# A two-layer decoder trunk on one core: the decay's inputs as columns ahead of the values', and stated places for k_d, low parts and adaLN dots

## The chip, the cores and the metric

The kernel runs on one core of a Trainium2 chip. The metric is the device time of one execution in microseconds (us). The engines are TensorE (PE; its weight loads are listed as PEld), VectorE (DVE), ScalarE (ACT), GpSimd (POOL) and SyncE (SP), which issues nearly all DMAs. Each engine runs its own instructions in a fixed order, and waits on semaphores for the others.

## The reference, cut to what matters

A trunk of two layers over 256 tokens of width 1024. Layer 0 mixes tokens by dilated window attention, layer 1 by gated linear attention; each is followed by a gated convolutional feed-forward part. Ahead of each sub-layer stands an RMSNorm whose shift, scale and gate come from a conditioning vector (adaLN: `silu(c) @ w_ada + b_ada`). The change lies in layer 1's mixer:

```python
def gla_mixer(h, w_in, w_gate, b_gate, g_norm, w_out):
    proj = h @ w_in                                  # q, k: 512 each, v: 1024, glr: 16, r: 1024
    ...
    gk = jax.nn.log_sigmoid((glr @ w_gate + b_gate).astype(jnp.float32)) / B_TAU
    ...
    bcum = jnp.cumsum(gk, axis=3)                    # within chunks of 64 tokens
    blast = bcum[:, :, :, -1:, :]
    q_t = q * jnp.exp(bcum)
    k_t = k * jnp.exp(-bcum)
    k_d = k * jnp.exp(blast - bcum)
    A = jnp.where(causal, jnp.einsum('bhncd,bhnsd->bhncs', q_t, k_t), 0.0)
    o_intra = jnp.einsum('bhncs,bhnse->bhnce', A, v)
    kv = jnp.einsum('bhncd,bhnce->bhnde', k_d, v)
    ...                                              # state over chunks: s = decay * s + kv
    o = o_intra + jnp.einsum('bhncd,bhnde->bhnce', q_t, s_prev)
    ...                                              # per head: rmsnorm(o) * silu(r), then @ w_out
```

There are four heads (key width 128, value width 256) and four chunks of 64 tokens.

## The kernel before

**Number format.** Large products run in F32R. Each float32 operand is split into a high part, a cast of it, and a low part, the rest. `mm3` (L196) makes one product of three: high × high, low × high, high × low (L199 to L201). `split` (L161) loads a weight piece into one of four raw buffers, casts the high parts on ScalarE (L172, tile whi, three buffers) and subtracts for the low parts on VectorE (L178, tile wlo, three buffers), each in two halves. Its arguments `after`, `low` and `late` name instructions behind which a half must stand.

**Order.** The program is recorded once; a scheduler then puts the instructions of each engine in order by its own estimate of times. `behind(...)` states that something must stand behind named instructions; everything else is the scheduler's. The order is fixed when the kernel runs.

**adaLN.** `next_ada` (L457) takes the next chunk of w_ada: one DMA of 1 MB into a raw buffer and two dots on VectorE (L140: one long operation and one that reads the accumulator), each followed by a small operation on ScalarE. The chunks in layer 1's mixer are for the feed-forward part behind it.

**Layer 1's mixer.** The normed input h stands as eight row blocks (kt) of 128 × 256, with a high part (hhi) and a low part (hlo) each; `all_normed` makes them from kt 0 to kt 7, while the first products already run. Then:

- *Values* (L1089 to L1109): the weight w_v_b comes in four pieces of two row blocks each, all 1024 columns wide. For each row block, each half of the tokens (t) and each half of the columns (s) there is an `mm3` into one of four PSUM banks pv[t][s].
- *Decay* (`log_gates`, L1045): behind the second piece a small weight w_glr (16 columns, padded) is split, and eight `mm3` give the 16 inputs as rows (tile glr, 16 × 256). `gates_of` (L1055) multiplies them by w_gate in plain float32, one product for each head (tile z), and makes log-sigmoid (nz, ea, sp), the running sum within chunks (cs), its distance from the chunk's end (dl), and the exponentials e_q, e_k, e_d and dec. It runs once for head 0 alone and once for heads 1 to 3 together.
- *Heads* (`states`, L1114): `mm3`s give q and k (bank pqk; for head 0 only k, since its q was made early), VectorE makes k_d, q_t and k_t, k_d is transposed (bank kdt) and copied (kdT), then come the masked scores (a, a_t) and three products kv, from which the states st follow. q_t, k_t, k_d have two buffers each, so head 3 takes those of head 1.
- *Outputs* (`products`, L1182, and `normed_output`, L1196): twenty small products (bank o) from a_t, v, q_t and st, their squares (osq, oacc), a mean over the head (ms, a product with a constant), and the normalised output on.
- *Output gate* (`gate`, L1211): four pieces of w_r_b (bank pr).

The order in which these are recorded:

```python
    s0 = states(0)
    s1 = states(1)
    output(0, *s0)
    s2 = states(2)
    po1 = products(1, *s1)
    s3 = states(3)
    normed_output(1, po1, last_a)
    po2 = products(2, *s2)
    gate(0)
    for _ in range(3):
        next_ada()
    po3 = products(3, *s3)
```

`last_a` is the last product of the scores, here head 3's: ms of head 1 stands behind it.

Of the kernel before, what the change touches and what calls it, by code (L numbers as in the profile page):

```python
# [57 lines left out]
def trunk(ctx: ExitStack, tc: tile.TileContext, I, out):  # L58
# [103 lines left out]
    def split(src, n, dmas=1, after=((), ()), late=(), low=(), lows=True):  # L162
# [5 lines left out]
        lo = wspl.tile([P, 2048], F32R, tag="wlo", name="wlo")  # L168
        for i in range(0, n, n // 2):
            c = slice(i, i + n // 2)  # L170
            with behind(*after[i > 0]):
                copied[0] = nc.scalar.copy(hi[:, c], raw[:, c])  # L172
        if not lows:
            return hi, lo, raw, n // 2
        for i in range(0, n, n // 2):
            c = slice(i, i + n // 2)
            with behind(*(late if i else low)):
                last_lo[0] = nc.vector.tensor_tensor(lo[:, c], raw[:, c], hi[:, c].bitcast(F32), op=ALU.subtract)  # L178
        return hi, lo
# [276 lines left out]

    def next_ada():  # L457
        if rest:
            ada_chunk(*rest.pop(0))

# [578 lines left out]
    nc.sync.dma_start(causal, I["causal"])  # L1039
    w_g = gt([16, 512], "w_g")  # L1040
    nc.sync.dma_start(w_g, I["w_gate"])

    glr_copy = []

    def log_gates():  # L1045
        with behind(*chain[5]):
            w_gl = split(I["w_glr"], 7 * 16 + P)
        ps = bank("glr", "t")
        for kt in range(KT):
            mm3(ps[:, :T], parts(w_gl, 16 * kt), h[kt], kt == 0, kt == KT - 1)  # L1050
        glr = gt([16, T], "glr")
        glr_copy.append(nc.vector.tensor_copy(glr, ps[:16, :T]))
        return [gates_of(*part, glr) for part in PARTS]

    def gates_of(first, n, glr):  # L1055
        def new(name, tag, columns=n * T):
            return gt([P, columns], name, tag=f"{tag}{min(first, 1)}")

        nz = new("nz", "A")
        for i in range(n):  # L1060
            hd = first + i
            ps = bank("z", "sttt"[hd])
            mm(ps[:, :T], w_g[:, P * hd : P * hd + P], glr, start=True, stop=True)
            nc.scalar.activation(nz[:, T * i : T * i + T], ps[:, :T], AF.Identity,
                                 scale=-1.0, bias=nbg[:, hd : hd + 1])
# [12 lines left out]
        dl = new("dl", "C")  # L1078
        nc.vector.tensor_tensor(dl.rearrange("p (n c) -> p n c", c=CH), cs3,
                                last.to_broadcast([P, 4 * n, CH]), op=ALU.subtract)  # L1080
# [9 lines left out]
    for n in range(4):  # L1090
        with behind(*((), chain[5], chain[7], glr_copy)[n]):
            w = split(I["w_v_b"][n], 2048) if n else w_first
            if n > 1:
                next_ada()
        if n == 0:
            with behind(*chain[7]):
                whole(early_q)
        for i in range(2):
            kt = 2 * n + i
            for t in range(2):  # L1100
                ht = [y[:, P * t : P * t + P] for y in h[kt]]
                for s in range(2):
                    mm3(pv[t][s], ht, parts(w, D * i + 512 * s, 512), kt == 0, kt == KT - 1)
        if n == 1:
            gates = log_gates()
    v = [gt([P, D], f"v{t}") for t in range(2)]
    for t in range(2):
        nc.scalar.copy(v[t][:, 0:512], pv[t][0])
        nc.vector.tensor_copy(v[t][:, 512:D], pv[t][1])  # L1109

    o_n = []
    last_a, last_sq, copies, kept = [None], [None], [None], [None, None]

    def states(hd):  # L1114
        if hd == 0:
# [5 lines left out]
        else:  # L1121
            w = split(I["w_qk_b"][hd], 2048)
            pqk = bank("pqk", "p")
# [10 lines left out]
        nc.vector.scalar_tensor_tensor(q_t, pq, P ** -0.5, e_q[:, c], op0=ALU.mult, op1=ALU.mult)  # L1134
        nc.vector.tensor_tensor(k_t, pk, e_k[:, c], op=ALU.mult)

        ps = bank("kdt", "t")
        kd = gt([P, T], "kdT", bufs=2)
        for t in range(2):
            c = slice(P * t, P * t + P)  # L1140
            nc.tensor.transpose(ps[:, c], k_d[:, c], ident)
        nc.scalar.copy(kd, ps[:, :T])
# [14 lines left out]
        vh = slice(T * hd, T * hd + T)  # L1157
        st = []
        kv = bank("kv", "t")
        for n in range(3):  # L1160
            t, r = n // 2, slice(CH * (n % 2), CH * (n % 2) + CH)
            d = (kv[:, :T], ps[:, T:], kv[:, T:])[n]
            last = mm(d, kd[r, P * t : P * t + P], v[t][r, vh], start=True, stop=True)
        if hd == 3:
# [16 lines left out]

    def products(hd, q_t, a_t, st):  # L1182
        po = bank("o", "s")
        for et in range(2):
            ev = slice(T * hd + P * et, T * hd + P * et + P)
            for t in range(2):
                d = po[:, T * et + P * t : T * et + P * t + P]
                mm(d, v[t][:, ev], a_t[:, t, :], start=True, stop=False)
                for n in range(2 * t, 2 * t + 2):
                    if n:  # L1190
                        last_o[0] = mm(po[:, T * et + CH * n : T * et + CH * n + CH],
                           st[n - 1][:, P * et : P * et + P], q_t[:, CH * n : CH * n + CH],
                           start=False, stop=(n % 2 == 1))
        return po
# [56 lines left out]
    gate(1)  # L1251
    next_ada()
    for n in range(4):
# [42 lines left out]
def _laid_out(a):  # L1296
# [49 lines left out]
    A["w_qk_b"][0] = wqk[:, :, :, 0].transpose(1, 2, 0, 3).reshape(P, 2048)  # L1346
    A["w_v_b"] = wb[:, 1024:2048].reshape(4, 2, P, D).transpose(0, 2, 1, 3).reshape(4, P, 2 * D)
    A["w_glr"] = wb[:, 2048:2064].reshape(KT, P, 16).transpose(1, 0, 2).reshape(P, KT * 16)
    A["w_glr"] = np.pad(A["w_glr"], ((0, 0), (0, P - 16)))
    A["w_r_b"] = pairs(wb[:, 2064:])  # L1350
    A["w_gate"] = a["w_gate_b"][0]
    s, t = np.arange(P)[:, None], np.arange(P)[None, :]
# [26 lines left out]
```

## Time and profile before

| | |
|---|---|
| Time, median of 3 runs | 765.04 us (764.12 to 766.68) |
| The profiled execution | 764.38 us |
| Its span, from the first to the last instruction | 762.6 us |
| Granted TensorE clock | 1.00 |
| HBM read | 184.43 MB |
| Layer 1's mixer up to the output gate | about 463 to 527 us of the span |

A line of the timeline gives the start in us, the length, engine, source line, operation, out<-in, shapes and a count; in brackets the idle time ahead of it and what ended it. A line of the chain of waits gives the start, the time that the piece sets, engine, tile and source line. A line of the busy times by stretch gives the stretch, its length, the busy time of PE, PEld, DVE, ACT and POOL (with counts), the granted clock, the DMA engines' share and GB/s. Matmuls are pipelined, so that the length of one is more than its pitch, the time from its start to the next one's. A product in plain float32 appears as two passes (x8 for four products).

### The profile page before, as it was taken

The numbers are of one execution on the slowest core, as the hardware profiler recorded it, in microseconds if no ns is written. First come the engines' busy times: TensorE is split into PE (matmuls) and PEld (weight loads), VectorE is DVE, ScalarE is ACT, GpSimd is POOL, SyncE is SP. The second block draws the span as 40 slices with busy tenths as digits, with TensorE's granted clock in tenths as the row PEclk, the third lists the DMA queues.
The fourth block names the chain that finished last, engine by engine and source line by source line (L and its number), as shares of the span: only waits on it lengthen the run. The fifth ranks groups of instructions, "written<-read, shape, count | busy, mean of one in ns | idle before, by whom it ended". The sixth has DMA issues, their size and how long they took to land.

```text
span 762.6 us, 16024 instructions
## 1 busy us (share of the span) xinstructions
PE 754.2 (99%) x6394; PEld 731.5 (96%) x6394; DVE 649.4 (85%) x1185; ACT 486.2 (64%) x951; POOL 33.6 (4%) x56
## 2 busy tenths in 40 slices
PE   8999999999999999999999999999999999999997
PEld 6999999999999999999999998899999999999997
DVE  6997999898989678999999778797668999998592
ACT  6476676565566478776777456746766866666551
POOL 0001101101101010000000000000010000000100
PEclk9999999999999999999999999999999999999999
DMA  9988889778787357878556976875356777774631
GB/s 348 404 287 312 318 293 325 281 256 307 285 275 254 112 198 257 319 262 277 202 172 234 340 263 228 305 275 178 132 190 216 241 269 271 209 174 157 200 104 56
DMA packets 39225, 186.57 MB, mean 245 GB/s; under 512 B 9004, under 2 KB 11820, under 8 KB 25070
## 3 DMA queue, kind: packets, MB, share of 16 engines
q1 hardware_dynamic: 38768, 185.10, 69.6%
q8 instruction: 50, 0.82, 0.4%
q10 hardware_dynamic: 382, 0.45, 0.2%
q14 instruction: 25, 0.20, 0.1%
HBM read 184.43 MB, written 1.10 MB: 243 GB/s over the span
## 4 chain that ended last, share of the span: by engine, by line
PE 94%; DVE 3%; DMA 2%; issue 1%; ACT 0%; DVEq 0%; ACTq 0%
PE pab L199 10%; PE pab L200 10%; PE pab L201 10%; PE pqk L199 5%; PE pd L199 5%; PE pd L200 5%; PE pd L201 5%; PE pqk L201 5%; PE pqk L200 5%; PE pv L199 3%; PE pv L200 3%; PE pv L201 3%; PE pqk L675 2%; PE py L199 2%; PE py L201 2%; PE py L200 2%
## 5 line engine op out<-in xcount | busy, mean ns | idle before, releaser
L172 ACT CAST whi<-raw 128x1024 fp32r<-128x1024 f32 (+4 forms) x262 | 237.7, 951 | 92.6 <-PE pab L200 35.5
L178 DVE TENSOR_TENSOR wlo<-raw,whi 128x1024 fp32r<-128x1024 f32 (+3 forms) x246 | 263.8, 1097 | 38.5 <-ACT whi L172 37.5
L200 PE MATMUL pab<-hlo,whi 128*128 128x256 f32 x672 | 184.6, 276 | 0.0
L201 PE MATMUL pab<-hhi,wlo 128*128 128x256 f32 x672 | 184.6, 276 | 0.0
L199 PE MATMUL pab<-hhi,whi 128*128 128x256 f32 x672 | 183.2, 277 | 0.0
L200 PEld LDWEIGHTS pab<-hlo,whi 128*128 128x128 f32 x672 | 126.0, 188 | 0.2
L201 PEld LDWEIGHTS pab<-hhi,wlo 128*128 128x128 f32 x672 | 126.1, 188 | 0.0
L199 PEld LDWEIGHTS pab<-hhi,whi 128*128 128x128 f32 x672 | 125.1, 188 | 0.1
L140 DVE CUSTOM_DVE_ANT_0 ada_raw<-ada_raw,c_bc 128x1024 f32<-128x1024 f32 x96 | 114.1, 1229 | 4.7 <-DMA ada_raw<-in_w_ada 4.7
L199 PE MATMUL pqk<-hhi,whi 128*128 128x256 f32 x356 | 98.0, 281 | 0.0
L200 PE MATMUL pqk<-hlo,whi 128*128 128x256 f32 x356 | 97.4, 279 | 0.0
L201 PE MATMUL pqk<-hhi,wlo 128*128 128x256 f32 x356 | 96.8, 279 | 0.2 <-DVE wlo L178 0.2
L200 PE MATMUL pd<-glo,whi 128*128 128x256 f32 x308 | 84.8, 276 | 0.0
L201 PE MATMUL pd<-ghi,wlo 128*128 128x256 f32 x308 | 84.8, 276 | 0.0
L199 PE MATMUL pd<-ghi,whi 128*128 128x256 f32 x308 | 84.7, 276 | 0.0
L201 PEld LDWEIGHTS pqk<-hhi,wlo 128*128 128x128 f32 x356 | 65.9, 188 | 1.1 <-issue 0.7
L200 PEld LDWEIGHTS pqk<-hlo,whi 128*128 128x128 f32 x356 | 66.7, 188 | 0.1
L199 PEld LDWEIGHTS pqk<-hhi,whi 128*128 128x128 f32 x356 | 66.5, 188 | 0.1
L200 PEld LDWEIGHTS pd<-glo,whi 128*128 128x128 f32 x308 | 57.7, 188 | 0.0
L201 PEld LDWEIGHTS pd<-ghi,wlo 128*128 128x128 f32 x308 | 57.7, 188 | 0.0
L199 PEld LDWEIGHTS pd<-ghi,whi 128*128 128x128 f32 x308 | 57.7, 188 | 0.0
L962 ACT ACTIVATE r<-pab,small 128x256 f32<-128x256 f32 x86 | 47.5, 561 | 7.0 <-DVE r L965 6.7
(269 smaller groups left out, 1498.8 us busy)
## 6 DMA issues: line engine op xcount, KB each, us to landing
raw<-in_w_up SPq DMA_DIRECT2D x42, 1024.0 KB, 4.9
ada_raw<-in_w_ada SPq DMA_DIRECT2D x29, 1024.0 KB, 5.8
raw<-in_w_down SPq DMA_DIRECT2D x28, 704.0 KB, 4.3
ada_raw<-in_w_ada SPq DMA_DIRECT2D x38, 512.0 KB, 6.8
raw<-in_wqk SPq DMA_DIRECT2D x18, 1024.0 KB, 6.9
raw<-in_wv SPq DMA_DIRECT2D x14, 768.0 KB, 6.5
raw<-in_w SPq DMA_DIRECT2D x7, 960.0 KB, 6.5
raw<-in_w_out_a SPq DMA_DIRECT2D x4, 1024.0 KB, 6.9
```

The lines of the kernel that those rows point to most:

```text
L140: i = nc.vector.tensor_tensor_reduce(w, w, c_bc, op0=ALU.mult, op1=ALU.add, scale=1.0, scalar=0.0, accum_out=dot,)
L172: copied[0] = nc.scalar.copy(hi[:, c], raw[:, c])
L178: last_lo[0] = nc.vector.tensor_tensor(lo[:, c], raw[:, c], hi[:, c].bitcast(F32), op=ALU.subtract)
L199: mm(ps, a[0], b[0], start=start, stop=False)
L200: mm(ps, a[0], b[1], start=False, stop=False)
L201: return mm(ps, a[1], b[0], start=False, stop=stop)
L675: mm(pqk[i], w[a], h[kt][b], start=s and i % 2 == 0 and (a, b) == (0, 0), stop=e and i % 2 == 1 and b == 1)
L962: nc.scalar.activation(r, u[:, :T], AF.Identity, scale=cw[2], bias=col(C_CB + 44 * l + f))
```

## The change

The 16 columns of the decay's inputs stand ahead of the first value columns, and the values are cut into three column groups (16 + 332, 346 and 346 columns) instead of four row pieces; each group has two weight pieces (row blocks 0 to 3 and 4 to 7), 1536 columns in storage. `split` gets a `view` that leaves the unused columns out. The first two groups' first halves are made before either second half.

The decay's inputs now come out with tokens on partitions. `stack_parts` puts three versions of them side by side (high part, low part, high part again), `turn_parts` transposes the two token halves, and `log_gates` multiplies the result, in F32R, by a w_gate of 128 rows which holds high, high and low parts at the matching rows: one F32R product for each head.

Order: the heads' low parts (head 2's) stand behind head 0's k_t; the running sums of heads 1 to 3 behind head 0's dl; the second half of head 1's products stands within head 3's states, between the transposes and the kv products; adaLN chunks in the mixer stand behind named instructions (in the value part behind the latest low part or the decay's copy, later behind k_t of head 1 and of head 3).

```diff
+VCUTS = ((0, 332), (332, 346), (678, 346))
+STACKED = (0, 32, 64)
...
-    def ada_chunk(l, n):
+    def ada_chunk(l, n, *after):
         raw = ada_load(l, n)
-        for s in range(2):
-            ada_dot(l, n, s, raw)
+        with behind(*after):
+            for s in range(2):
+                ada_dot(l, n, s, raw)
...
+    def columns(n, half, **order):
+        c = (348, 346, 346)[n]
+        return split(I["w_v_b"][n, half], 4 * 384, view=lambda w: w.rearrange("p (k c) -> p k c", k=2)[:, :, 0:c], **order)
...
     with behind(*sixth):
-        w_first = split(I["w_v_b"][0], 2048, late=last_x[1:])
+        w_first = [columns(0, 0, late=last_x[:1]), columns(1, 0, low=last_x[1:], late=last_x[1:])]
...
+    def stack_parts(pv):
+        for t in range(2):
+            hi, lo, again = (stacked[:, t, at : at + 16] for at in STACKED)
+            ps = pv[t][:, 0:16]
+            nc.vector.tensor_copy(hi, ps)
+            nc.vector.tensor_tensor(lo, ps, hi.bitcast(F32), op=ALU.subtract)
+            nc.vector.tensor_copy(again, hi.bitcast(F32))
+
+    def turn_parts():
+        ps = bank("glr", "t")
+        for t in range(2):
+            last = nc.tensor.transpose(ps[:, P * t : P * t + P], stacked[:, t, :].bitcast(F32), ident)
+        low_rank.append(nc.vector.tensor_copy(glr, ps[:, 0:T]))
+        return last
...
-        w_gl = split(I["w_glr"], 7 * 16 + P)
-        for kt in range(KT):
-            mm3(ps[:, :T], parts(w_gl, 16 * kt), h[kt], kt == 0, kt == KT - 1)
+                last = mm(sums_of[hd], w_g[:, P * hd : P * hd + P], glr, start=True, stop=True)
...
-        nc.vector.scalar_tensor_tensor(sp, nz, 0.0, ea, op0=ALU.max, op1=ALU.add)
+        with behind(*offsets):
+            nc.vector.scalar_tensor_tensor(sp, nz, 0.0, ea, op0=ALU.max, op1=ALU.add)
...
+    values(0, 0, w_first[0])
+    last = values(1, 0, w_first[1])
+    with behind(*chain[3]):
+        w = columns(0, 1)
+    last = values(0, 1, w, after=[last])
...
+    stack_parts(pv[0])
+    with behind(*chain[7]):
+        w = columns(1, 1)
+        next_ada(last_lo[0])
+    last = values(1, 1, w, range(2), [last])
+    with behind(last):
+        last = turn_parts()
+    keep_values(0)
+    last = values(1, 1, w, range(2, 4), [last])
+    with behind(last):
+        last = log_gates()
...
-            w = split(I["w_qk_b"][hd], 2048)
+            w = split(I["w_qk_b"][hd], 2048, **(dict(low=first_kt[:1], late=first_kt[:1]) if hd == 2 else {}))
...
+        ahead = between(last_kd)
...
-    po1 = products(1, *s1)
-    s3 = states(3)
-    normed_output(1, po1, last_a)
+    s3 = states(3, ahead)
+    normed_output(1, po1[0], last_a)
     po2 = products(2, *s2)
     gate(0)
-    for _ in range(3):
-        next_ada()
+    for i in (1, 3):
+        next_ada(first_kt[i])
...
     gate(1)
-    next_ada()
+    for _ in range(2):
+        next_ada(first_kt[3])
```

More of the change, by code (lines that the diff above doesn't have):

```diff
@@ L171, in split @@
             with behind(*after[i > 0]):
-                copied[0] = nc.scalar.copy(hi[:, c], raw[:, c])
+                copied[0] = nc.scalar.copy(part(hi[:, c]), part(raw[:, c]))
         if not lows:
@@ L455, in trunk, with next_ada @@
     rounds, first_loads = [0], []
-    def next_ada():
+    def next_ada(*after):
         if rest:
-            ada_chunk(*rest.pop(0))
+            ada_chunk(*rest.pop(0), *after)
     def next_half(after):
@@ L1039, in trunk, with gates_of @@
     nc.sync.dma_start(causal, I["causal"])
-    w_g = gt([16, 512], "w_g")
-    nc.sync.dma_start(w_g, I["w_gate"])
-    glr_copy = []
-    def log_gates():
-        with behind(*chain[5]):
-            w_gl = split(I["w_glr"], 7 * 16 + P)
-        ps = bank("glr", "t")
-        for kt in range(KT):
-            mm3(ps[:, :T], parts(w_gl, 16 * kt), h[kt], kt == 0, kt == KT - 1)
[L1051 to L1055, printed above, removed]
+    w_g = gt([P, 512], "w_g", F32R)
+    w_raw = gt([P, 512], "w_raw", tag="C1")
+    nc.sync.dma_start(w_raw, I["w_gate"])
+    with behind(*chain[7]):
+        nc.scalar.copy(w_g, w_raw)
+        own = slice(STACKED[2], STACKED[2] + 16)
+        nc.vector.tensor_tensor(w_g[own, :], w_raw[own, :], w_g[own, :].bitcast(F32), op=ALU.subtract)
+    stacked = gt([P, 2, P], "stacked", F32R)
+    nc.gpsimd.memset(stacked.bitcast(F32), 0.0)
+    glr = gt([P, T], "glr", F32R)
+    sums_of, low_rank, offsets = [], [], []
+    def stack_parts(pv):
[11 more added lines that the diff above has]
+        return last
+    def log_gates():
+        for tg in "st":
+            ps = bank("z", tg)
+            for i in range(2):
+                hd = len(sums_of)
+                sums_of.append(ps[:, T * i : T * i + T])
+                last = mm(sums_of[hd], w_g[:, P * hd : P * hd + P], glr, start=True, stop=True)
+        return last
+    def gates_of(first, n):
         def new(name, tag, columns=n * T):
@@ L1089, in trunk @@
     pv = [[bank("pv", tg) for _ in range(2)] for tg in "ps"]
[L1090 to L1093, printed above, removed]
-                next_ada()
[L1095 to L1105, printed above, removed]
@@ L1106, in trunk, with values @@
-    v = [gt([P, D], f"v{t}") for t in range(2)]
[L1107 to L1111, printed above, removed]
+    v = [gt([P, D], f"v{t}") for t in range(2)]
+    def values(n, half, w, kts=range(4), after=()):
+        c = (348, 346, 346)[n]
+        for j in kts:
+            kt = 4 * half + j
+            with behind(*after):
+                for t in range(2):
+                    ht = [y[:, P * t : P * t + P] for y in h[kt]]
+                    last = mm3(pv[n][t][:, 0:c], ht, parts(w, 384 * j, c), kt == 0, kt == KT - 1)
+        return last
@@ new lines, in keep_values @@
+    def keep_values(n):
+        first, c = VCUTS[n]
+        at = 0 if n else 16
+        for t, copy in enumerate((nc.scalar.copy, nc.vector.tensor_copy)):
+            copy(v[t][:, first : first + c], pv[n][t][:, at : at + c])
+    values(0, 0, w_first[0])
[3 more added lines that the diff above has]
+    last = values(0, 1, w, after=[last])
+    with behind(*chain[7]):
+        whole(early_q)
+    stack_parts(pv[0])
+    with behind(*chain[7]):
+        w = columns(1, 1)
+        next_ada(last_lo[0])
@@ new lines, in trunk @@
+    last = values(1, 1, w, range(2), [last])
[5 more added lines that the diff above has]
+        last = log_gates()
+    pv.append([bank("pv", "t") for _ in range(2)])
+    gates = [gates_of(*part) for part in PARTS]
+    with behind(*low_rank):
+        w = columns(2, 0)
+        next_ada(last_lo[0])
+    keep_values(1)
+    last = values(2, 0, w, after=[last])
+    w = columns(2, 1)
+    values(2, 1, w, after=[last])
@@ L1134, in states @@
         nc.vector.scalar_tensor_tensor(q_t, pq, P ** -0.5, e_q[:, c], op0=ALU.mult, op1=ALU.mult)
-        nc.vector.tensor_tensor(k_t, pk, e_k[:, c], op=ALU.mult)
+        first_kt.append(nc.vector.tensor_tensor(k_t, pk, e_k[:, c], op=ALU.mult))
         ps = bank("kdt", "t")
@@ L1162, in states @@
             d = (kv[:, :T], ps[:, T:], kv[:, T:])[n]
-            last = mm(d, kd[r, P * t : P * t + P], v[t][r, vh], start=True, stop=True)
+            with behind(*ahead):
+                last = mm(d, kd[r, P * t : P * t + P], v[t][r, vh], start=True, stop=True)
         if hd == 3:
@@ L1180, in output, with products @@
         normed_output(hd, products(hd, *state))
-    def products(hd, q_t, a_t, st):
+    def products(hd, q_t, a_t, st, last=None):
         po = bank("o", "s")
@@ L1185, in products @@
             ev = slice(T * hd + P * et, T * hd + P * et + P)
[L1186 to L1193, printed above, removed]
+            with behind(*([last] if last and et else [])):
+                for t in range(2):
+                    d = po[:, T * et + P * t : T * et + P * t + P]
+                    mm(d, v[t][:, ev], a_t[:, t, :], start=True, stop=False)
+                    for n in range(2 * t, 2 * t + 2):
+                        if n:
+                            last_o[0] = mm(po[:, T * et + CH * n : T * et + CH * n + CH],
+                               st[n - 1][:, P * et : P * et + P], q_t[:, CH * n : CH * n + CH],
+                               start=False, stop=(n % 2 == 1))
         return po
@@ L1233, in trunk, with ahead @@
     s2 = states(2)
-    po1 = products(1, *s1)
-    s3 = states(3)
-    normed_output(1, po1, last_a)
+    po1 = []
+    def ahead(turned):
+        po1.append(products(1, *s1, last=turned))
+        return last_o
+    s3 = states(3, ahead)
+    normed_output(1, po1[0], last_a)
     po2 = products(2, *s2)
     gate(0)
-    for _ in range(3):
-        next_ada()
+    for i in (1, 3):
+        next_ada(first_kt[i])
     po3 = products(3, *s3)
```

33 lines of the change are left out of this document (19 added, 14 removed).

## The prediction

> **What bounds the kernel now.** I read the page first, for the share of each engine and the chain that ended last, and then the busy time of the engines in the stretches that the edits touch.
>
> ```profile
> span 762.6 us, 16024 instructions
> PE 754.2 (99%) x6394; PEld 731.5 (96%) x6394; DVE 649.4 (85%) x1185; ACT 486.2 (64%) x951; POOL 33.6 (4%) x56
> PE 94%; DVE 3%; DMA 2%; issue 1%; ACT 0%; DVEq 0%; ACTq 0%
> ...
> 463.34:490.74 27.40, 27.40 (x132) 22.53 (x131) 22.88 (x39) 19.76 (x41) 0.00 (x0) 1.00 0.84 320
> 490.74:522.21 31.47, 31.47 (x251) 29.21 (x249) 27.48 (x48) 15.89 (x36) 0.62 (x2) 1.00 0.64 231
> 522.21:526.52 4.31, 4.31 (x33) 3.88 (x34) 3.90 (x8) 3.82 (x6) 0.00 (x0) 1.00 0.00 0
> ```
>
> The three stretches are the values and decay, the heads up to the products of head 1, and the rest up to the output gate. TensorE is busy for the whole of each, at a granted clock of 1.00, and 94% of the chain is TensorE. So nothing else sets the time there: a matmul taken out is worth its pitch (start to start), and any new wait of TensorE is paid in full. The pitches come from the chain of waits and the timeline of TensorE:
>
> ```profile
> 474.85 0.28 PE L201 MATMUL glr<-hhi,wlo 128*128 128x256 f32 x1
> ...
> 477.44 0.39 PE L199 MATMUL pv<-whi,hhi 128*128 128x512 f32 x1
> ...
> 477.61 0.93 PE pv L199 x4
> ...
> 482.43 0.23 PE pv L199
> 482.66 1.92 PE z L1063 x8
> 484.58 0.43 PE pv L200
> 485.01 0.24 PE pv L201
> ...
> 490.74 0.12 PE pqk L199
> ...
> 499.23 0.22 PE kdt L1141 x2
> 499.44 0.45 PE a L1152 x4
> ...
> 240.04 0.18 PE pv L200
> ...
> 241.26 0.17 PE pv L201
> ```
>
> Between the first two rows stand 22 products of 256 columns: 2.59 / 22 = 0.118 us. Four of 512 columns take 0.93: 0.2325, call it 0.231 with the single rows. The last two rows, of the attention stage, are seven steps of 384 columns apart: 1.22 / 7 = 0.174.
>
> **The change, part by part.** *Decay's inputs as columns.* The 24 products of glr go: 24 × 0.118 = −2.83. The 96 value products of 512 columns become 48 of 348 and 96 of 346. No row has this width. Bounds: 384's row in proportion (346/384 × 0.174 = 0.157) and 384's row whole (0.174). I take the line through 256 and 512 (0.118 + 90 × 0.113/256 = 0.158), which lies at the near end: 144 × 0.158 = 22.75 against 96 × 0.231 = 22.18, +0.57, and at the far end +2.9.
>
> *The decay product.* z was four products in plain f32, two passes each (x8): 1.92, and 0.20 more in the value product behind it, 0.43 against 0.23. In F32R it is four products of 256 columns, 0.47: −1.65. New are two transposes of `stacked`, priced by kdt's row at 0.22, plus a switch from F32R to f32 and back, which the same 0.20 prices: +0.42. I count two more such switches in the new order of TensorE's instructions among the heads, because products of head 0's and 1's outputs stand apart: +0.4 (up to +0.8, if entering costs as much as leaving).
>
> TensorE's own sum: −2.83 + 0.57 − 1.65 + 0.42 + 0.4 = −3.1.
>
> *Side work.* Six weight pieces of 768 KB replace four of 1 MB, the 120 KB piece of w_glr goes and w_gate grows from 32 to 256 KB: about 0.6 MB more, 2 us of the queues at the window's 320 GB/s, over a stretch where their share is 0.84; the pieces stand one or more groups ahead of their use, as before. w_gate and causal now stand on SP behind the fourth value piece, which waits only for a low part of the first; w_gate is wanted at z, far behind. The low parts stay about equal (12 × some 0.79 against 8 × 1.14 and two small ones). New on VectorE are six copies of 16 columns and w_gate's low part of 512 columns, all inside the 4.5 us (27.40 − 22.88) that VectorE has free there.
>
> ```profile
> 459.80 0.38 DVE L1026 TENSOR_SCALAR nbg<-small 128x4 f32<-128x4 f32 x1
> 459.87 1.22 DVE L178 TENSOR_TENSOR wlo<-raw,whi 128x1024 fp32r<-128x1024 f32 x1
> ...
> 496.85 0.42 DVE L1133 TENSOR_TENSOR k_d<-pqk,e_d 128x256 f32<-128x256 f32 x1
> ```
>
> The six copies have one tight place: they stand behind an adaLN chunk on VectorE, and TensorE wants them for its transposes 12 value products (1.9 us) after the group that they read. A small operation takes between 0.07 (the pitch of nbg) and 0.38 (its whole length), six 0.4 to 2.3, with two dots (2.3, below) ahead of them: TensorE waits 0 to 0.6 there. I take 0.2, since most of the dots run before the group ends.
>
> The first head's chain keeps its cover. Before, k_d starts 496.85 − 482.66 = 14.2 after z and is used at 499.23, 2.0 after its end. Now z comes at 463.34 + 96 × 0.158 + 0.42 = 478.9, and kdt behind z (0.5), 48 value products (7.6) and 72 of pqk (8.5, as between 490.74 and 499.23) at 495.5; k_d done 14.6 after z is 493.5. Two us of cover are left; without them each us late is a us lost.
>
> *The dots' stated places.* This is where I expect the gain to go. In the new order VectorE has, right behind k_t of head 3, four dots (two adaLN chunks), and only then oacc of head 1, which TensorE's ms waits for. Before, nothing stood between.
>
> ```profile
> 521.81 0.39 PE o L1191 x4
> 522.21 0.41 PE kv L1163
> ...
> 523.26 0.64 PE a L1152 x4
> 523.90 0.43 PE ms L211 x2
> 524.34 0.22 PE o L1188 x2
> ...
> 526.52 0.17 PE pr L199
> ...
> 522.24 0.42 DVE L1134 SCALAR_TENSOR_TENSOR q_t<-pqk,e_q 128x256 f32<-128x256 f32 x1 [0.90 <-PE o L1191]
> 522.59 0.41 DVE L1135 TENSOR_TENSOR k_t<-pqk,e_k 128x256 f32<-128x256 f32 x1
> 522.91 0.41 DVE L1200 TENSOR_TENSOR oacc<-osq 128x256 f32<-128x256 f32 x1
> 523.71 0.48 DVE L1172 SCALAR_TENSOR_TENSOR st<-st,dec,kdt 128x256 f32<-128x256 f32 x1 [0.38 <-ACT st L1170]
> ...
> 524.83 3.49 DVE L178 TENSOR_TENSOR wlo<-raw,whi 128x1024 fp32r<-128x1024 f32 x3
> ...
> 498.38 1.22 DVE L140 CUSTOM_DVE_ANT_0 ada_raw<-ada_raw,c_bc 128x1024 f32<-128x1024 f32 x1
> ...
> 500.67 2.35 DVE L178 TENSOR_TENSOR wlo<-raw,whi 128x1024 fp32r<-128x1024 f32 x2
> ```
>
> q_t of head 3 cannot start earlier: it waits for the end of head 1's products (o, 522.21), whose buffer it takes, and the new program keeps that wait. In before's clock: q_t at 522.24, k_t at 522.59, the dots from 522.91; two dots took 500.67 − 498.38 = 2.29, so four end at 527.49 and oacc at 527.90. TensorE has kv (1.05) and a (0.64) until 523.90 and then stands at ms until about 527.95 (0.05 for the hand-over, an estimate from the 0.03 between o and q_t): **+4.05**. Both chunks have landed by then: by the new order the buffers that they take come free at head 2's low parts and at the chunk behind head 0's mask, ahead of head 2's products. Behind ms on TensorE stand head 2's outputs and the whole gate, so all of the wait counts. Next late would be st, a_t, st (523.71 to 524.83, 1.1) and the gate's first low part (some 1.15): done at 530.2, while TensorE needs it after ms and o (524.34 to 526.52) at 527.95 + 2.62 = 530.6 or later. So nothing further is late.
>
> The sum: −3.1 + 0.2 + 4.05 = **+1.1**. The profiled execution took 764.38 us, its span 762.6 and 1.8 around it: 765.5. The three runs shown have a median of 765.04, 0.66 above the profiled one, so I forecast 765.04 + 1.1 = **766.1**.
>
> **Rivals.** *The wait at ms isn't paid* (faster). Should TensorE come to ms 4 us later than the last products of head 1, or oacc come ahead of the dots, the sum is −3.1 + 0.2: 762.1. For it: every pitch in TensorE's sum has its row. Against it: the order of VectorE's instructions is fixed, and between o and ms the rows show 1.69 us of work.
>
> *TensorE's clock falls in the wait* (slower). Before never leaves TensorE idle after its start, and at that start it is slow:
>
> ```profile
> 2.24 3.76 PE cb L123 x4
> ...
> 11.33 1.40 PE rows L405 x6
> ```
>
> The first four passes of 512 columns take 1.84 ns a column, the later six (2 × 512 and 4 × 128 columns) 0.91. If a wait of 4 us brings that state back, ms and o behind it (523.90 to 526.52) take 2.6 us more: 768.7. It decides only if the wait is long enough for the clock. [...]
>
> *A cover among the first head's steps is lost* (slower): the casts that now stand ahead of the sigmoid's first step on ScalarE, or a weight piece that lands late, push k_d past its 2.0 us of cover. One to two us beyond it: 766.1 + 1.5 = 767.6. For it: four value groups' casts and w_qk_b's share ScalarE and the queues with that chain. Against: the same chain with two casts of 1024 columns in it took 14.2 before.
>
> **How the numbers follow.** Chances: the forecast 0.5, no wait at ms 0.2, the clock 0.13, a lost cover 0.17. The range is 761.8 to 769.0: down to the first rival, up to the clock's case, which takes in the far ends of the value products and the switches (+2.3, +0.4). The forecast's own range is 764.6 to 768.9. A measurement of this kernel tells about 0.3% (2.3 us) from no change: 762.7 and 767.3. Faster holds the first rival, 0.2. Slower holds the clock, most of the lost cover and a part of the forecast's upper range: 0.13 + 0.12 + 0.13 = 0.38. The rest, 0.42, is no change that can be told.
>
> **What would show it.** TensorE's stretch from the first value product to kdt should be 3.4 to 3.5 shorter, with pitches of 0.158; z a row of about 0.47 for four. Behind o of head 1, ms should wait about 4 us for VectorE's oacc, with four dots straight ahead of it; the chain of waits should pass through these dots, and TensorE's busy share fall in that stretch. Shorter first products and no idle time at ms would make the forecast wrong on the fast side; pitches near 0.17, passes at double length behind ms, or idle time ahead of the stacked transposes or of kdt on the slow side.

## The result and the profile after

The changed kernel takes 770.06 us (median of 6 runs, 768.56 to 771.54) against 764.68 (median of 6, 764.12 to 766.68) for the kernel before in the same comparison: a ratio of 1.0069, with a 95% interval of 1.0058 to 1.0079. It is slower by 5.4 us, where 1.1 was forecast.

The page of the changed kernel, with its span, its engines, the granted clock in 40 slices and the chain that ended last:

```profile
span 768.2 us, 16085 instructions
PE 755.2 (98%) x6416; PEld 737.0 (96%) x6416; DVE 650.9 (85%) x1195; ACT 485.5 (63%) x955; POOL 33.6 (4%) x57
...
PE   8999999999999999999999999997999999999997
...
PEclk9999999999999999999999999997999999999999
...
PE 90%; DVE 6%; ACT 3%; issue 1%; DMA 0%; DVEq 0%; ACTq 0%
```

The stretches of layer 1 (start and end, length, busy time of TensorE, its weight loads, VectorE, ScalarE and GpSimd with their instructions, granted clock, share and rate of the queues), from 520.04 on cut at the edges of the clock's steps:

```profile
463.14:487.50 24.36, 24.36 (x158) 24.32 (x157) 22.33 (x45) 19.34 (x43) 0.00 (x0) 1.00 0.76 283
487.50:518.31 30.81, 30.81 (x247) 28.29 (x245) 21.96 (x39) 13.15 (x27) 0.62 (x2) 1.00 0.47 182
...
520.04:523.45 3.41, 0.00 (x0) 0.00 (x0) 3.41 (x7) 3.41 (x8) 0.00 (x0) 1.00 0.26 53
523.45:526.87 3.42, 2.72 (x11) 2.58 (x12) 3.42 (x8) 1.31 (x4) 0.00 (x0) 0.50 1.02 417
526.87:530.28 3.41, 3.41 (x18) 3.41 (x18) 3.41 (x5) 0.49 (x1) 0.00 (x0) 0.50 1.01 408
530.28:533.69 3.41, 3.41 (x18) 3.41 (x18) 3.41 (x6) 2.54 (x6) 0.00 (x0) 0.50 1.04 377
533.69:537.10 3.41, 3.41 (x31) 3.41 (x31) 0.51 (x2) 0.00 (x0) 0.00 (x0) 1.00 0.98 363
```

One slice of 19 us shows a 7 both for TensorE and for its clock. The stretches say why: from 520.04 to 523.45 TensorE does nothing at all, and from 523.45 to 533.69, three stretches of 3.41 us, it works at a granted clock of 0.50: 18 products in each full stretch, against 31 in the next one at 1.00.

The chain that ended last in order of time, from decay's transposes to ms:

```profile
476.84 0.22 PE glr L1072 x2
478.95 0.48 PE z L1082 x4
...
495.24 0.22 PE kdt L1196 x2
...
517.90 0.41 PE o L1249 x4
...
518.33 0.42 DVE q_t L1189
...
522.52 1.14 DVE ada_raw L142
...
524.15 1.19 PE ms L215 x2
```

VectorE's instructions in the same place and TensorE's ms (start, length, engine, line, operation, tiles, shape, count; in brackets the idle time before and who ended it):

```profile
493.39 0.41 DVE L1188 TENSOR_TENSOR k_d<-pqk,e_d 128x256 f32<-128x256 f32 x1
...
518.67 0.41 DVE L1190 TENSOR_TENSOR k_t<-pqk,e_k 128x256 f32<-128x256 f32 x1
519.00 1.21 DVE L142 CUSTOM_DVE_ANT_0 ada_raw<-ada_raw,c_bc 128x1024 f32<-128x1024 f32 x1
...
522.44 1.22 DVE L142 CUSTOM_DVE_ANT_0 ada_raw<-ada_raw,c_bc 128x1024 f32<-128x1024 f32 x1
...
523.58 0.42 DVE L1258 TENSOR_TENSOR oacc<-osq 128x256 f32<-128x256 f32 x1
...
524.15 1.19 PE L215 MATMUL ms<-oacc,ones_d 128*128 128x256 f32 x2 [4.15 <-DVE oacc L1258]
```

Where before the chain stayed on TensorE, it now leaves it at 518.31 for VectorE: four dots stand from 519.00 to 523.58 between k_t and oacc, and ms waits 4.15 for oacc. The time adds up so, each against its row of before: TensorE ends the products of head 1 at 518.31 instead of 522.21, −3.9 (0.2 of it had been gained ahead of the values). Then +4.15 for the wait, and half of the work done at half clock, (2.72 + 3.41 + 3.41) / 2 = +4.77. Together +5.0; the spans differ by 768.2 − 762.6 = 5.6. Of the other 0.6, 0.5 arises in the last 12 us: the 90 products from the first transposes at the program's end (y) to the last one of the down projection (pd) take 749.74 to 761.71, 11.97, instead of 744.72 to 756.22, 11.50. TensorE waits for nothing there, and it isn't the change's doing: the same stretch takes 11.50 in the run kept at work and 11.97 in the run with both chunks in idle time, both below.

### The profile page after: what moved, and what is told of

Read it like the earlier page. It is cut to its first block, busy times and chain, and to the rows that moved or that the text cites. A ratio compares the mean times of both kernels' runs of the same rounds, so it can differ in the third digit from the quotient of the medians.

```text
span 768.2 us, 16085 instructions
## 1 busy us (share of the span) xinstructions
PE 755.2 (98%) x6416; PEld 737.0 (96%) x6416; DVE 650.9 (85%) x1195; ACT 485.5 (63%) x955; POOL 33.6 (4%) x57
## 4 chain that ended last, share of the span: by engine, by line
PE 90%; DVE 6%; ACT 3%; issue 1%; DMA 0%; DVEq 0%; ACTq 0%
PE pab L204 10%; PE pab L203 10%; PE pab L205 10%; PE pd L204 5%; PE pd L203 5%; PE pd L205 5%; PE pqk L203 5%; PE pqk L205 5%; PE pqk L204 5%; PE pv L203 4%; PE pv L205 4%; PE pv L204 4%; DVE ada_raw L142 2%; PE py L203 2%; PE py L205 2%; PE py L204 2%
## 5 line engine op out<-in xcount | busy, mean ns | idle before, releaser
L182 DVE TENSOR_TENSOR wlo<-raw,whi 128x1024 fp32r<-128x1024 f32 (+5 forms) x248 | 263.8, 1089 | 36.4 <-ACT whi L176 35.6
L203 PE MATMUL pv<-whi,hhi 128*128 128x384 f32 (+2 forms) x160 | 53.2, 337 | 0.3 <-ACT v L628 0.3
```

What stands on the lines that cost most here:

```text
L182: last_lo[0] = nc.vector.tensor_tensor(part(lo[:, c]), part(raw[:, c]), part(hi[:, c].bitcast(F32)), op=ALU.subtract)
L203: mm(ps, a[0], b[0], start=start, stop=False)
```

## The experiments

The theory was a wait at ms of 4.1 us, a clock at half behind it, and TensorE's own gain of 3.7. "Half stretches" below are stretches of 3.41 us at half clock. In a program of some 762 us each takes 3.41 / 2 / 762 = 0.0022 off the mean granted clock, so they can be counted for each execution: 0.998 to 1.000 is none (as in all runs of the kernel before in these comparisons), 0.996 to 0.997 one, 0.994 to 0.995 two, 0.991 to 0.993 three. The readings within a class differ because the clock falls once more behind TensorE's last product, where it costs nothing: in the 13 profiled executions the last 0.4 to 3.2 us of the span, 0.0003 to 0.0021. So 0.993 can also be two. The six runs of the changed kernel lie at 0.991 to 0.993: three half stretches in five of them, and three or two in the one at 0.993 (768.56, the fastest).

Each edit also lets the scheduler place anew what isn't stated. In the runs with the dots later, with one, two or three dots, kept at work and in VectorE's idle time, TensorE's order up to ms of head 1 is that of the changed kernel (but for the added products); in the other runs it isn't.

**The dots later.** The order that the change states is kept, but the two chunks go behind the first low part of the gate's weights (of which a handle is kept).

```diff
+    gate_low = low_of[0]
-    for i in (1, 3):
-        next_ada(first_kt[i])
+    next_ada(first_kt[1])
+    next_ada(gate_low)
...
-        next_ada(first_kt[3])
+        next_ada(gate_low)
```

> The changed kernel, with the two chunks' four dots stated behind the gate's first low part instead of behind k_t of head 3; oacc of head 1 stands directly behind k_t again. Theory (wait at ms, and a clock that falls in it): ms waits for nothing to speak of, the granted clock stays at 1.00 through the gate, and what is left is TensorE's gain of 3.7: 764.7 - 3.7 = 761.0. Rival (VectorE is simply late by four dots somewhere, clock or not): the dots cost their 4 us behind the gate's low part instead, TensorE waits for a low part of the gate or of w_qkv there: 764 to 766. Rival (the columns themselves cost the time): no change against the changed kernel, 770.

Measured: 762.2 (ratio to the kernel before 0.9966, 0.9954 to 0.9979), 7.9 below the changed kernel. That is 1.2 above the 761.0 expected. One wait of TensorE is left in that part (waits: who for whom, in total, times, longest), and the clock is whole:

```profile
PE ms L215 <- ACT ln L217: 0.6, 1, 0.6
```

The stretches from that part's a to the gate's products:

```profile
518.99:525.00 6.01, 6.01 (x52) 5.96 (x52) 5.63 (x10) 5.14 (x10) 0.00 (x0) 1.00 0.33 104
525.00:535.00 10.00, 10.00 (x88) 9.95 (x88) 9.71 (x16) 6.33 (x14) 0.00 (x0) 1.00 1.01 386
```

Wait and clock are gone together, and with them all of the loss. In the new place 0.6 of wait is left, behind the four dots. The rival with the columns at fault is out.

**Two dots.** Only one chunk stays ahead of oacc; the others stand behind the low part as above.

```diff
+    gate_low = low_of[0]
     for i in (1, 3):
         next_ada(first_kt[i])
...
-        next_ada(first_kt[3])
+        next_ada(gate_low)
```

> The changed kernel with only one chunk (two dots) left between k_t of head 3 and oacc of head 1, the other behind the gate's first low part. Theory: the wait at ms is 4.15 - 2.29 = 1.9, too short for the clock, which stays at 1.00: 761.0 + 1.9 = 762.9. Rival (the extra time beyond the wait is in proportion to the wait, as with work that is late behind the dots): half of 4.15 + 4.65, so 761.0 + 4.4 = 765.4.

Measured: 766.04 (763.01 to 768.18 in 11 runs; ratio 1.001, 0.9997 to 1.0023). My number was wrong by 3.1. The wait came out as worked out, as the timeline of TensorE shows, but the clock fell:

```profile
521.82 1.19 PE L215 MATMUL ms<-oacc,ones_d 128*128 128x256 f32 x2 [1.86 <-DVE oacc L1258]
```

The stretches on the clock's grid:

```profile
517.97:521.38 3.41, 2.00 (x13) 1.35 (x12) 3.17 (x8) 2.62 (x4) 0.27 (x1) 1.00 0.00 0
521.38:524.80 3.42, 2.98 (x12) 2.83 (x13) 3.42 (x6) 2.58 (x7) 0.00 (x0) 0.50 0.65 220
524.80:528.21 3.41, 3.41 (x18) 3.41 (x18) 3.41 (x6) 0.97 (x4) 0.00 (x0) 0.50 0.99 389
```

In the stretch ahead of the fall TensorE had worked 2.00 of 3.41 us, and was idle in one piece of 1.42 at its end. Nothing like a whole stretch was idle. The 11 executions differ: three at a clock of 0.999 took 763.01, 763.13 and 764.41, where 762.9 was expected without a fall; two with one half stretch took 765.5 and 765.9; four with two, 766.0 to 767.7; one with three 768.2, and one at 0.993, with two or three, 766.5. The same program, the same work ahead of oacc; what can change from run to run is where the wait lies among the stretches, whose edges do lie elsewhere in each profiled execution (523.45 in the changed kernel, 521.38 here); that this decides is not shown. The rival's 765.4 was nearer to the median, but for a reason that the spread excludes: lateness in proportion would be the same in every run.

**TensorE kept at work in the wait.** Dots as in the changed kernel, 18 added products on TensorE between a and ms.

```diff
     s3 = states(3, ahead)
-    normed_output(1, po1[0], last_a)
+    warm = bank("warm", "p")
+    with behind(*last_a):
+        for _ in range(18):
+            last_warm = mm(warm[:, :P], ones_d, ones_d, start=True, stop=True)
+    normed_output(1, po1[0], [last_warm])
```

> The changed kernel with its four dots where they are, and 18 products of ones by ones (128 columns, plain f32, into a bank that nothing reads) added on TensorE behind the last product of a, so that it works during most of the wait at ms. Theory: ms starts when it did (524.2 and at most 0.5 later), but the clock stays at 1.00 behind it, so the 4.65 of the half clock go: 770.1 - 4.65 = 765.4, at most 766. Rival (the rest of the time is late work of VectorE and not the clock): 769 to 770.5.

Measured: 766.17 (765.27 to 768.3; ratio 1.0018, 1.0008 to 1.0028), all nine runs at a clock of 0.998 or above; at most 766 was expected. In the timeline of TensorE the added products end where ms begins:

```profile
521.19 4.18 PE L1302 MATMUL warm<-ones_d 128*128 128x128 f32 x36
525.50 0.67 PE L215 MATMUL ms<-oacc,ones_d 128*128 128x256 f32 x2
```

The stretch behind it:

```profile
525.50:535.00 9.50, 9.49 (x82) 9.45 (x83) 9.50 (x15) 4.16 (x8) 0.00 (x0) 1.00 1.02 398
```

ms comes no earlier than the dots let it (this execution was 1.4 later than the changed kernel's already in layer 0), yet it takes 0.67 instead of 1.19, and useless work made the program 3.9 faster. So 3.9 of the 5.4 are the clock's, shown by itself; the rival of late work on VectorE, which is as late here, is out.

**The dots in the kernel before.** Nothing of the change but two chunks behind k_t of head 3 (and one behind that of head 1), and oacc behind the last dot.

```diff
     s3 = states(3)
-    normed_output(1, po1, last_a)
+    ahead = []
+    for i in (1, 3, 3):
+        ahead = next_ada(first_kt[i])
+    normed_output(1, po1, last_a, [ahead])
```

> The kernel before, with nothing of the change but the four dots stated between k_t of head 3 and oacc of head 1. Theory: a wait of about 4.1 at ms and then some 9 us at half clock, so 764.7 + 4.1 + 4.65 = 773.4, with a granted clock of 0.5 for about 10 us behind the wait. Rival (the wait alone): 768.8. Rival (the loss needs the rest of the change): 764.7 to 766.

Measured: 771.96 (769.29 to 772.93; ratio 1.0088, 1.0072 to 1.0104). ms in the timeline of TensorE:

```profile
526.39 1.22 PE L213 MATMUL ms<-oacc,ones_d 128*128 128x256 f32 x2 [2.91 <-DVE oacc L1203]
```

Two stretches on the clock's grid:

```profile
521.47:524.88 3.41, 1.77 (x10) 1.20 (x10) 3.41 (x7) 2.44 (x6) 0.00 (x0) 1.00 0.17 19
524.88:528.29 3.41, 1.90 (x7) 1.73 (x8) 3.41 (x7) 2.78 (x8) 0.00 (x0) 0.50 0.86 346
```

The loss needs nothing else of the change: all five runs lie at a clock of 0.991 to 0.997. The wait at ms is 2.9 here and not the 4.1 expected, because the scheduler put the products of head 1 ahead of kdt of head 3; before, they stand between kdt and kv (519.76 to 522.13), and TensorE waits for neither k_d nor kdT. Here it waits 0.5 for each of these and comes to ms later; 2.9 + 1.0 + (1.90 + 3.42 + 3.41) / 2 = 8.3 against the 7.8 by which the spans differ.

**One dot and three dots.** The same edit as with two, with one dot, then three, ahead of oacc; the chunk with the odd dot is split, its second dot behind the low part.

```diff
+    with behind(first_kt[3]):
+        ada_dot(l, n, 0, raw)
+    with behind(gate_low):
+        ada_dot(l, n, 1, raw)
```

> The changed kernel with one dot left between k_t of head 3 and oacc of head 1, the other three behind the gate's first low part. The wait at ms is 4.15 - 3 x 1.15 = 0.7. In the run with two dots a wait of 1.86 brought the clock down in most executions, for two stretches of 3.41 us, so the first theory of a full idle stretch has fallen. Theory now (the clock is set anew every 3.41 us by how much of the stretch before TensorE worked; 0.7 of 3.41 idle is too little): 762.2 + 0.7 = 762.9 with a clock of 1.00. Rival (any wait brings it down): 762.9 + 1.7 for each stretch at half clock, 764.6 to 766.3.

> The changed kernel with three of the four dots left between k_t of head 3 and oacc of head 1, the fourth behind the gate's first low part: a wait of 4.15 - 1.15 = 3.0, shorter than one stretch of 3.41 us. Theory (the clock is set every 3.41 us by the share of the stretch before in which TensorE worked; 3.0 idle always leave one stretch with too little work): two or three stretches at half clock, each 3.41 / 2 = 1.7 us lost: 761.5 + 3.0 + 3.4 to 5.1 = 767.9 to 769.6, in every execution a clock below 1.00. Rival (a whole stretch has to be idle): 761.5 + 3.0 = 764.5 at a clock of 1.00.

Measured: one dot 762.56 (761.24 to 763.44, 11 runs, all at 0.998 or above); three dots 767.24 (765.35 to 770.98, 12 runs, all at 0.997 or below). The first as expected; of the second the median lies 0.7 below the range, since half of its runs had only one half stretch. The wait with one dot, in the timeline of TensorE:

```profile
520.60 0.67 PE L215 MATMUL ms<-oacc,ones_d 128*128 128x256 f32 x2 [0.71 <-DVE oacc L1258]
```

The stretch around it and the next:

```profile
519.78:523.20 3.42, 2.71 (x23) 2.58 (x22) 3.42 (x8) 3.35 (x6) 0.00 (x0) 1.00 0.00 0
523.20:526.61 3.41, 3.41 (x32) 3.41 (x31) 3.41 (x7) 2.05 (x6) 0.00 (x0) 1.00 0.87 288
```

The two stretches on either side of the fall with three dots:

```profile
519.51:522.92 3.41, 1.67 (x10) 1.09 (x10) 3.41 (x7) 2.94 (x5) 0.00 (x0) 1.00 0.00 0
522.92:526.33 3.41, 2.15 (x8) 2.00 (x9) 3.41 (x8) 2.52 (x8) 0.00 (x0) 0.50 0.84 271
```

The waits at ms and the half stretches, by dots ahead of oacc:

| dots | wait at ms, us | median, us | runs with 0 / 1 / 2 / 3 half stretches |
|---|---|---|---|
| 0 | none for oacc | 762.2 | 5 / 0 / 0 / 0 |
| 1 | 0.7 | 762.56 | 11 / 0 / 0 / 0 |
| 2 | 1.9 | 766.04 | 3 / 2 / 4 or 5 / 2 or 1 |
| 3 | 3.0 | 767.24 | 0 / 6 / 3 / 3 |
| 4 | 4.15 | 770.06 | 0 / 0 / 0 or 1 / 6 or 5 |

A wait of 3.0 is shorter than a stretch and brought the clock down in all 12 executions. That a whole stretch must be idle is excluded.

**Bursts of work in the wait.** Behind each of the first three dots TensorE multiplies the dot's own output, two products or four, so that the idle time comes in pieces.

```diff
+                with behind(*last_a):
+                    for i in range(2):
+                        last_warm = mm(warm[:, :P], raw[:, D * s + P * i : D * s + P * i + P], ones_d, start=True, stop=True)
```

> The changed kernel with its four dots ahead of oacc, and behind each of the first three of them two products on TensorE (128 columns, plain f32, of the dot's own output, into a bank that nothing reads), about 0.46 us; the chunks are issued ahead of the output of head 1, which moves some products of the heads among each other. The wait of 4.15 becomes pieces of 0.7, 0.7 and 1.25 with work between them; TensorE works some 1.4 of the 4.15. Theory (the share of work in a stretch counts): a stretch of 3.41 holds some 60% idle time, more than the 35 to 42% that brought the clock down with two dots, so it falls as in the changed kernel: 768 to 771. Rival (the length of one idle piece counts; 0.7 with one dot left it up): the clock stays at 1.00: 770.1 - 5.1 = 765.0.

> As the run with bursts of two products, with four products in each burst: 0.92 of each 1.15 us at work, idle pieces of 0.2 to 0.3 and one of 0.8 ahead of ms. Theory (share): idle at most some 1.0 of a stretch of 3.41, about 30%, at the edge of what brought the clock down: mostly at 1.00, 765 to 766.5. Rival (any work of this kind, plain f32 products of 128 columns, doesn't count in full): the clock falls, 768 or more.

Measured: 767.51 (766.44 to 768.51) and 765.83 (765.32 to 768.8). The clock stayed at 0.998 or above in all but one run of 5 (0.996) and in all 11. With two products, the timeline of TensorE:

```profile
519.98 0.71 PE L1311 MATMUL warm<-ones_d,ada_raw 128*128 128x128 f32 x4 [0.29 <-DVE dot L142]
...
522.27 0.71 PE L1311 MATMUL warm<-ones_d,ada_raw 128*128 128x128 f32 x4 [0.43 <-DVE dot L142]
523.84 0.67 PE L215 MATMUL ms<-oacc,ones_d 128*128 128x256 f32 x2 [0.86 <-DVE oacc L1259]
```

The emptiest stretch around the wait, and two stretches at the end of the same execution:

```profile
521.90:525.32 3.42, 2.19 (x16) 1.98 (x16) 3.42 (x9) 2.40 (x9) 0.00 (x0) 1.00 0.74 240
...
757.42:760.84 3.42, 1.88 (x18) 1.64 (x16) 1.64 (x5) 1.45 (x4) 0.00 (x0) 1.00 0.16 62
760.84:764.25 3.41, 0.00 (x0) 0.00 (x0) 0.09 (x1) 0.00 (x0) 0.00 (x0) 1.00 0.40 154
```

My number for the theory failed, and the run doesn't decide between the two: a burst takes 0.71 in the record and not 0.46, so the emptiest stretch (counted on the grid from the edge at which the clock first rose) still had 2.19 of work, more than the 2.00 that lost the clock. Around the wait, share of work in a stretch (lost at 2.00 of 3.41 and below, kept at 2.19 and above) and length of the idle piece both fit. The end of the program fits neither: the stretch with 1.88 of work, whose idle piece of 1.55 reaches to its end, left the clock at 1.00, and it fell only behind the next one, without work. The two-dot run lost it behind more recorded work (2.00) and a shorter piece (1.42). So neither of the two, as these records measure them, draws the line. The busy time of the weight loads (the second one in a line) does so far, 1.35 and less lost and 1.64 and more kept, but no run varied it by itself. The median lies 2.5 above the rival's 765 with the clock whole, the profiled execution (766.44) 1.4: 1.2 of that is a new wait at the sum of squares near the program's end. The rest I didn't trace. With four products the time is as the theory said, and that of the run kept at work throughout.

**The columns alone.** The heads' order, the chunks' places and all of the stated orders as before; the columns, transposes and the F32R product as changed.

```diff
-            w = split(I["w_qk_b"][hd], 2048, **(dict(low=first_kt[:1], late=first_kt[:1]) if hd == 2 else {}))
+            w = split(I["w_qk_b"][hd], 2048)
...
-        with behind(*offsets):
-            nc.vector.scalar_tensor_tensor(sp, nz, 0.0, ea, op0=ALU.max, op1=ALU.add)
+        nc.vector.scalar_tensor_tensor(sp, nz, 0.0, ea, op0=ALU.max, op1=ALU.add)
...
-    s3 = states(3, ahead)
-    normed_output(1, po1[0], last_a)
+    s3 = states(3)
+    normed_output(1, po1, last_a)
...
-    for i in (1, 3):
-        next_ada(first_kt[i])
+    for _ in range(3):
+        next_ada()
```

> The changed kernel with the columns and the decay product as changed, but with the heads' order, the chunks' places and the output of head 1 as in the kernel before (nothing stated). Theory (the columns give TensorE 3.7 back, the loss comes from the stated places alone): no wait at ms, clock 1.00 throughout, 765.0 - 3.7 = 761.3, at most 762. Rival (the first head's chain needs its stated order, without which k_d is late): 763 to 765, with TensorE waiting at kdt.

Measured: 767.84 (765.49 to 769.55; ratio 1.0034, 1.0022 to 1.0047). The theory failed and the rival held, more strongly than it said. TensorE's waits in the heads:

```profile
PE kdt L1195 <- DVE k_d L1187: 3.1, 1, 3.1
PE kv L1219 <- ACT kdT L1196: 0.7, 1, 0.7
```

VectorE's instructions ahead of k_d:

```profile
494.66 2.36 DVE L182 TENSOR_TENSOR wlo<-raw,whi 128x1024 fp32r<-128x1024 f32 x2
...
498.13 0.42 DVE L1187 TENSOR_TENSOR k_d<-pqk,e_d 128x256 f32<-128x256 f32 x1
```

The stretch that holds most of the wait, and the one behind it:

```profile
496.26:499.67 3.41, 1.06 (x8) 0.94 (x9) 3.41 (x6) 1.46 (x3) 0.00 (x0) 1.00 1.00 399
499.67:503.08 3.41, 3.41 (x17) 3.20 (x16) 3.41 (x8) 0.87 (x3) 0.00 (x0) 0.50 0.64 216
```

Low parts of later weights (2.36) and the distances of heads 1 to 3 stand ahead of k_d, whose e_d was done at 495.38; k_d starts at 498.13 (493.39 in the changed kernel), TensorE waits 3.1 and 0.7, and a half stretch follows: 761.5 + 3.8 + 1.7 = 767.0. Of the 12 runs nine lie at a clock of 0.994 to 0.997; the three at 0.998 and above took 765.49 to 766.49, near the 761.5 + 3.8 = 765.3 of the waits alone. So the order that the change states for the heads earns its place, and of the stated places the dots' ahead of oacc lose. Which of the stated orders undone here (head 2's low parts, the running sums, head 1's products, the chunks) does it, I did not separate.

**The dots in VectorE's idle time.** In the run with the dots later VectorE stood idle from 510.9 to 514.8, behind oacc of head 0. One chunk goes there, then both.

```diff
-        nc.vector.tensor_tensor(acc, sq[:, 0:T], sq[:, T : 2 * T], op=ALU.add)
+        first_acc.append(nc.vector.tensor_tensor(acc, sq[:, 0:T], sq[:, T : 2 * T], op=ALU.add))
...
-        next_ada(first_kt[i])
+        next_ada(first_acc[0])
```

> The changed kernel with one of the two chunks behind oacc of head 0 (VectorE stood idle from 510.9 to 514.8 in the run with the dots behind the gate's low part), the other behind the gate's first low part. Theory: the 2.3 us in the gap cost nothing, the other two dots less than the four did there (0.6 us of wait at the ms of head 2 fall to 0): 761.0 to 761.9. Rival (the rest of that run's 762.2 has another source): 762.2 as it was.

> As the run with one chunk in the gap, but both chunks' four dots there: 4.6 us of work in 3.9 us of idle time, so a_t of head 1 comes 0.6 to 0.7 later, and TensorE, which took a_t 0.5 after its end, waits up to 0.2. Theory: 761.0 to 761.5, clock 1.00 throughout. Rival (the chunks have not landed by 511, VectorE waits for them and everything behind is late): a wait of some us at o of head 1, and the clock falls with it: 765 or more.

Measured: 761.8 (ratio 0.9958, 0.9942 to 0.9974) and 761.46 (0.9956, 0.9943 to 0.9969). In neither does TensorE wait anywhere from the values to the end of the gate. VectorE with both chunks there:

```profile
511.24 0.41 DVE L1258 TENSOR_TENSOR oacc<-osq 128x256 f32<-128x256 f32 x1
511.57 1.22 DVE L142 CUSTOM_DVE_ANT_0 ada_raw<-ada_raw,c_bc 128x1024 f32<-128x1024 f32 x1
...
516.15 0.44 DVE L1208 COPY_PREDICATED a_t<-causal,a 128x256 f32<-128x256 uint32 x1
```

Both kernels are faster than the one before, by 0.4%, and than the changed one by 8 us. They can't be told from each other.

## Why the prediction was wrong

- *TensorE's own sum* was right, and a little small. From the first value product to kdt it is now 495.24 − 463.14 = 32.10 instead of 499.23 − 463.34 = 35.89: 3.8 shorter where 3.4 to 3.5 were said. (The prediction's own walk through that stretch, with kdt at 495.5, gives 3.7; its sum didn't take that over.) The value products come 0.158 apart in the chain of waits, as said; z takes 0.48 (0.47 said), the transposes 0.22. The two further switches among the heads, put at 0.4, can have cost only about 0.1, as the products of head 1 still end 3.7 earlier by the same count. The stacked transposes waited for nothing (0.2 taken).
- *The first head's chain* kept its cover: k_d done at 493.80, kdt at 495.24, 1.4 where 2.0 were said. The columns alone show what it depends on: without the stated orders TensorE waits 3.1 for k_d.
- *The wait at ms* was right in place, cause and size: 4.05 said, 4.15 measured, the chain of waits through four dots, nothing late behind it.
- *The step that failed is the clock behind the wait*: the sum has no term for it, because the prediction made it a rival, "TensorE's clock falls in the wait", and had that wrong in its condition and in its price. The condition I took, that a whole stretch must be idle, and with it the chance of 0.13, rested on nothing that a run here shows. The fall came in 6 runs of 6, and a wait of 1.9 sufficed in 8 of 11. In the profiled execution of the changed kernel a whole stretch of 3.41 us was idle; with two and three dots none was, with 2.00 and 1.67 us of work in the stretch ahead of the fall. The price was 2.6, ms and o of head 2 alone at double length. Measured is 4.77: the slow clock ran on into the gate's products, to 533.69, over 9.54 us of work. With the fall in the sum at its measured price, 766.1 + 4.8 = 770.9, within the runs' 768.56 to 771.54. That it fits so well is in part luck: TensorE's gain was 0.6 larger than its sum and the 0.2 at the stacked transposes did not come, while 0.1 of wait and 0.5 at the program's end came on top.
- "Before never leaves TensorE idle after its start" is not exact: it waits three times, 0.8 us in all and at most 0.3 each, ahead of layer 1's mixer, and its granted clock stays at 1.00 there.
- *A lost cover* and *no wait at ms* did not happen.

Why two dots lose the clock in some executions and not in others is shown only as far as the counts go. What exactly the clock goes by (neither recorded work nor the idle piece in a stretch draws the line, 1.88 with a piece of 1.55 kept and 2.00 with 1.42 lost), and what decides whether one, two or three half stretches follow, stay open.

## What to carry to other kernels

In these runs a new wait of 1.9 to 4.15 us on TensorE, at work throughout otherwise, was not priced by its length: half clock could follow it, 1.7 us for each stretch of 3.41, none to three of them behind 1.9 and one to three behind 3.0 and more. Price a wait of that length both with the half clock and without it. A wait of 0.7 left the clock up in 11 runs of 11 (762.56 against 762.2 without the wait). Before stating a place for side work, list what stands right behind it on its engine and who waits for that; the same four dots cost 8.6 us ahead of oacc of head 1 (770.06 against 761.46) and nothing that shows 7 us earlier, in idle time of the same engine. And split a change before judging it: the stated orders of the heads are worth some 6 us where the dots stand well (767.84 against 761.46), the stated place of the dots costs 8.6.

## What the runs showed of the hardware that was not expected

- In the traces the granted clock changed only at the edges of a grid of 3.41 us (in the changed kernel at 523.45, 533.69 and 765.80, 3 and 68 stretches apart), which lies elsewhere in each profiled execution (the fall is at 521.38 with two dots, at 522.92 with three). It fell behind stretches with 0.00, 1.06, 1.67, 1.77 and 2.00 us of work, and not behind stretches with 1.88 (at a program's end), 2.19 and 2.71.
- Once down, it stayed down for one stretch (behind 1.06 us of work, followed at once by dense work), two (behind 2.00) or three (behind 0.00, 1.67 and 1.77). In the changed kernel TensorE worked all of the second and third.
- A program's own spread can come from this: 763.0 to 768.2 for two dots, with none to three half stretches at 1.7 us each, and no change in the order.
